# A hybrid decoder layer: block sums of right operands and the residual added by accumulating DMA on GpSimd's queue instead of VectorE

## The chip, the cores and the metric

The kernel runs on one core of one Trainium2 chip. The metric is the device time of one execution in microseconds (us). The engines are named as the profile names them: PE is TensorE (PEld its weight loads), DVE is VectorE, ACT is ScalarE, POOL is GpSimd, SP is SyncE, which here only issues DMAs. PSUM is the memory that TensorE writes, SBUF the working memory of 128 partitions. DMAs issued by SP are on the queue that the profile calls hardware_dynamic, those issued by POOL on the one called software_dynamic.

## The reference: what is computed

One layer of a decoder for one sequence of 1024 rows and a width of 2048, in float32, followed by a last RMSNorm. Cut to what matters here:

```python
h = rmsnorm(x, ln_g)                     # (1024, 2048)
proj = h @ w_in                          # one input projection, split into the groups' columns
out_a = gmlp_spatial_gating(g_u, g_v, ...) * silu(g_z)             # width 512
out_b = rmsnorm(gated_delta_rule(q, k, v, g, beta)) * silu(d_z)    # width 1024
out_c = cross_attention(c_q, mem) * silu(c_z)                      # width 512
mixed = concatenate([out_a, out_b, out_c])                         # (1024, 2048)
x = x + mixed @ w_out                    # the residual input is added here
return rmsnorm(x, final_g)
```

## The kernel before

**Precision and products.** Every large float32 product is made of three matmuls in the type float32r: each operand is split into a high part (a cast on ACT, `whi`, `zh` or `ahi`) and a low part (value minus high part, a subtraction on DVE, `wlo`, `zl` or `alo`), and `triple` adds high x high, high x low and low x high in PSUM.

**Order of the work.** Nothing is issued where it is written. Each call of an engine is recorded by `Plan.add` with what it depends on (reads and writes of tiles and DRAM tensors). `Plan.price` gives it a cost and, for DMAs, a size and a latency. `Plan.issue` then simulates the engines with these numbers and a rank (`with rank(...)`; smaller goes first) and emits the instructions in the order of the simulated start times. So all instructions carry the line of that emission, L274 in the profile, and each engine works through a fixed list in order. An instruction that waits holds up all that stand behind it on its engine; this goes for SP's and POOL's DMAs too.

**Stages.** The memory tokens' keys and values come first. Then come two passes (`half`) over the 512-row halves, which project q, k and v for the gated delta rule and run its chunked scan. Last come five products in block form, each made by `seven`: three input projections (`project_pair` 0, 1 and 2, for the gates, the queries and gMLP's u) and two output projections (`out_pair` 0 and 1, two 512-column blocks of `w_out` each).

**The block form.** The rows (two halves), the inner dimension (two halves of eight 128-blocks) and the columns (two 512-column blocks) give a 2 x 2 by 2 x 2 block product. `seven` computes it with seven block products instead of eight, from sums of blocks of the left operand (activations) and of the right one (weights). The products come in the order m = 1, 7, 6, 4, 5, 3, 2. Each runs over eight 128-blocks j in pairs, with four PSUM tiles t per block: 8 x 4 x 3 = 96 matmuls of 512 columns. After each product, `take1` to `take7` add what stands in PSUM to the results `y[half, column block]` on DVE. The left sums lie in DRAM (`s_d`); they were made in the background by `left_sums` and by `mix_done`, which adds on POOL.

**The right operand.** For `project_pair` 0 the sums of weight blocks are made ahead, in the background of the first `half`, by `right_sums` (L738). A job takes four 512-column blocks from `w_in` into four `zg` tiles (SP), makes four differences on DVE and stores them to `t_d` (SP). There are eight jobs, at rank 6, started at marks in the projections (`next_job`). For the other four block products `rights_made` (L1241) makes the sums as they are needed: it loads one weight block per j into one of two buffers `wraw2` (through `plain`). For m = 1, 2 and 3 that is the operand. For m = 7 it also loads block (1,1) into a kept tile and subtracts on DVE; for m = 6 it adds to the kept tile; for m = 4 and 5 it subtracts the kept tile from the loaded block, in the buffer. Then `split2` makes the high and low parts.

**Residual and norm.** In `out_pair`, `take6` and `take4` call `add_x` (L1470): a 512-column piece of x is loaded into one of six tiles (`xin`: the tiles `E` and `tn`) and added to `y` on DVE. `square` (ACT) sums the squares of a finished piece, `close` takes the root (a power on POOL), scales and stores the rows.

Of the kernel before, what the change touches and what calls it, by code (L numbers as in the profile page):

```python
# [17 lines left out]
P = 128  # L18
# [44 lines left out]
class Plan:  # L63
# [117 lines left out]
    def price(self, o, name, outs, ins):  # L181

        out = outs[0]
        n = math.prod(out.shape[1:])
        both = [*outs, *ins]
        psum = any(i.space == PSUM for i in both)
        pointer = any(i.shape[-1] == 1 and math.prod(i.shape[1:]) == 1 for i in ins[1:])
        o.nbytes = o.lock = 0
        o.lat = 0.0
        if name == "dma_start":  # L190
            o.cost = {"sp": 380.0, "act": 100.0, "pool": 800.0}[o.eng]
            rows = math.prod(out.shape[:-1])
            o.nbytes = max(4 * math.prod(out.shape), 512 * rows)
            src = ins[0]
            pieces = src.shape[-1] < 128 or out.shape[-1] < 128
            if out.space == DRAM:
                o.lat = 700.0 if pieces else 0.0
            elif pieces or list(src.ap)[0][0] == 0:
                o.lat = 2400.0
        elif o.eng == "pe":  # L200
            passes = 1 if ins[0].dtype == F32R else 2 if name == "transpose" else 4
            o.cost = max(13.3 + n / 2.4 * passes, 24.0 * out.shape[0] / 32 if out.shape[0] < P else 0.0)
            o.lat = 175.0
        elif o.eng == "act":
            o.cost = (165.0 if psum else 200.0) + 0.82 * n + (105.0 if pointer else 0.0)
            o.cost += 190.0 if "accum_out" in o.kw else 0.0
        elif o.eng == "dve":
            n = max([n] + [math.prod(i.shape[1:]) for i in ins])
            o.cost = (n + 151) / 0.96 + (60.0 if pointer and name == "scalar_tensor_tensor" else 0.0)
            o.lock = not psum and (name.startswith("tensor_") or name == "scalar_tensor_tensor")  # L210
            o.lock = o.lock and name != "tensor_reduce"
        else:
            o.lock = 1
            if name in ("memset", "affine_select"):
                o.cost = 100.0 + 0.83 * n * (1 if name == "memset" else 1.4)
            else:
                o.cost = 550.0 + 150.0 * (n - 1) if n < 8 else 200.0 + 2.1 * n
# [60 lines left out]
def kernel(  # L278
# [447 lines left out]
    def left_sums(src, dst):  # L726
        a, b, c, d = (ring["zg"]() for _ in range(4))
        with rank(6):
            for t, x_ in zip((a, b, c, d), src):
                Q.dma_start(t, x_)  # L730
            V.tensor_tensor(out=d, in0=c, in1=d, op=ALU.add)
            V.tensor_tensor(out=c, in0=a, in1=c, op=ALU.subtract)
            V.tensor_tensor(out=a, in0=d, in1=a, op=ALU.subtract)
            V.tensor_tensor(out=b, in0=b, in1=a, op=ALU.subtract)
            for t, x_ in zip((d, a, c, b), dst):
                Q.dma_start(x_, t)

    def right_sums(src, dst):  # L738
        a, b, c, d = (ring["zg"]() for _ in range(4))
        with rank(6):  # L740
            for t, x_ in zip((a, b, c, d), src):
                Q.dma_start(t, x_)
            V.tensor_tensor(out=a, in0=b, in1=a, op=ALU.subtract)
            V.tensor_tensor(out=b, in0=d, in1=b, op=ALU.subtract)
            V.tensor_tensor(out=d, in0=d, in1=a, op=ALU.subtract)
            V.tensor_tensor(out=c, in0=c, in1=d, op=ALU.subtract)
            for t, x_ in zip((a, d, b, c), dst):
                Q.dma_start(x_, t)

    def blk(w, k, c0):  # L750
        return w[k * P : (k + 1) * P, c0 : c0 + HT]
# [401 lines left out]
    ah4, al4 = (over([t.rearrange("p t k c -> p (t k c)")[:, i * 2 * HT : (i + 1) * 2 * HT] for t in ts for i in range(2)])  # L1153
                for ts in (ahq[0:2], alq[0:2]))
    wraw2 = over(kvraw[:2])
    more = [[ring["inv"]()]]
    whi3 = over([*kvhi, heir(zgb[0], "zh", "zg0", 2 * HT, F32R)])
    wlo3 = over([*kvlo, heir(zgb[1], "zl", "zg1", 2 * HT, F32R)])
    ywide = [heir(o, f"y{i}", tag)
# [20 lines left out]
                split_to(hi[:, i * n : (i + 1) * n], lo[:, i * n : (i + 1) * n], t, V)  # L1180
        return hi, lo

    def add(o, a, b):
        with rank(1):
            V.tensor_tensor(out=o, in0=a, in1=b, op=ALU.add)

    def seven(lefts, rights, banks, plan, order=range(NH), rows=False, last=False):

        for n, (m, take) in enumerate(plan):
# [22 lines left out]
                    product(t, *h)  # L1212
                take(t, bank[t])
            if n == 1:
                araw.bufs[1:] = more


    def lefts(blocks, s):
# [21 lines left out]

    def rights_made(blocks, kept):  # L1241


        def get(m, js):
            r = plain([blocks(*((0, 0), (1, 0), (1, 1), (1, 0), (1, 1), (0, 0), (0, 1))[m - 1], j) for j in js])
            if m < 4:
                return split2([r], whi3(), wlo3())
            ts = kept[js[0] // 2]
            if m == 7:
                with rank(4):  # L1250
                    for i, x_ in enumerate(js):
                        t = ts[i] if len(ts) == 2 else ts[0][:, i * HT : (i + 1) * HT]
                        Q.dma_start(t, blocks(1, 1, x_))
            with rank(2):
                for i, t in enumerate(ts):
                    n = t.shape[1]
                    x_ = r[:, i * n : (i + 1) * n]
                    if m in (4, 5):
                        V.tensor_tensor(out=x_, in0=x_, in1=t, op=ALU.subtract)
                    else:  # L1260
                        V.tensor_tensor(out=t, in0=t, in1=x_, op=ALU.subtract if m == 7 else ALU.add)
            return split2([r] if m in (4, 5) else ts, whi3(), wlo3())

        return get

# [8 lines left out]
    def project_pair(c, ys, done, kept=None, first=3):  # L1274

        y = {k: ys[4 * i : 4 * i + 4] for i, k in enumerate(KEYS)}

        def fin(key, t):
            with rank(first if key[0] == 1 else 3):
                done(*key, t, y[key][t])  # L1280

        def take1(t, a):
            with rank(1):
                S.copy(y[0, 0][t], a)

        def take7(t, a):
            add(y[1, 1][t], a, y[0, 0][t])

        def take6(t, a):
            add(y[1, 1][t], a, y[1, 1][t])  # L1290
            add(y[0, 1][t], a, y[0, 0][t])

        def take4(t, a):
            add(y[1, 0][t], a, y[1, 1][t])
            fin((1, 0), t)

        def take5(t, a):
            add(y[1, 1][t], a, y[1, 1][t])
            add(y[0, 1][t], a, y[0, 1][t])
            fin((1, 1), t)  # L1300

        def take3(t, a):
            add(y[0, 1][t], a, y[0, 1][t])
            fin((0, 1), t)

        def take2(t, a):
            add(y[0, 0][t], a, y[0, 0][t])
            fin((0, 0), t)

        def w_block(i, b, j):  # L1310
            return blk(w_in, NH * i + j, pairs[c][b])

        plan = ((1, take1), (7, take7), (6, take6), (4, take4), (5, take5), (3, take3), (2, take2))
        right = rights_made(w_block, kept) if kept else rights_kept(w_block, t_d)
        seven(lefts(h_block, s_d[0]), right, lambda n: wide, plan)


# [28 lines left out]
    def mix_done(hf, k, y):  # L1346
# [4 lines left out]
        with rank(6):  # L1351
            if hf == 0:
                Q.dma_start(a, s_d[1][j][1])
                G.tensor_tensor(out=a, in0=y, in1=a, op=ALU.subtract)
                Q.dma_start(s_d[1][j][3], a)
                return
            c, d = spare_t(), spare_t()
            Q.dma_start(a, mix_d[0][set1[j]])
            Q.dma_start(c, mix_d[1][set1[j]])
            G.tensor_tensor(out=d, in0=c, in1=y, op=ALU.add)  # L1360
            G.tensor_tensor(out=c, in0=a, in1=c, op=ALU.subtract)
            G.tensor_tensor(out=a, in0=d, in1=a, op=ALU.subtract)
            for i, t in enumerate((d, a, c)):
                Q.dma_start(s_d[1][j][i], t)

# [74 lines left out]
    fg = [t[:, i * HT : (i + 1) * HT] for t in fg for i in range(2)]  # L1440
    for c in range(4):
        Q.dma_start(fg[c], final_g[c * HT : (c + 1) * HT].partition_broadcast(P))
    xin = Ring("", 0, None)
    xin.bufs = ring["E"].bufs + ring["tn"].bufs
    ssy = [[small() for _ in range(NT)] for _ in range(2)]
    ys = [[[None] * 4 for _ in range(NT)] for _ in range(2)]

# [19 lines left out]
                    to = S  # L1467
            to.dma_start(out[r0 : r0 + P, c * HT : (c + 1) * HT], y)

    def add_x(half_, t, c, a=None):  # L1470
        y, r0 = ys[half_][t][c], half_ * HT + t * P
        xt = xin()
        Q.dma_start(xt, x[r0 : r0 + P, c * HT : (c + 1) * HT])
        add(y, y if a is None else a, xt)

    def square(half_, t, c):
        S.activation(jk, ys[half_][t][c], AF.Square, accum_out=ssy[half_][t][:, c : c + 1])
# [1 line left out]
    def out_pair(cp, slots, kept):  # L1479
# [11 lines left out]
            add(y[1, 1][t], a, y[0, 0][t])  # L1491

        def take6(t, a):
            add(y[1, 1][t], a, y[1, 1][t])
            add(y[0, 1][t], a, y[0, 0][t])
            add_x(0, t, c1)
            add_x(0, t, c2)

        def take4(t, a):
            add(y[1, 0][t], a, y[1, 1][t])  # L1500
            add_x(1, t, c2)
            add_x(1, t, c1)
            square(1, t, c1)

        def take5(t, a):
            add(y[1, 1][t], a, y[1, 1][t])
            add(y[0, 1][t], a, y[0, 1][t])
            square(1, t, c2)
            if cp == 1:
                close(1, t)  # L1510

        def take3(t, a):
            add(y[0, 1][t], a, y[0, 1][t])
            square(0, t, c2)
            G.tensor_tensor(out=y[0, 1][t], in0=y[0, 1][t], in1=fg[c2], op=ALU.mult)
            if cp == 1:
# [57 lines left out]
```

## Time and profile before

| what | value |
| --- | --- |
| median of 3 runs | 1705.58 us (1704.8 to 1708.16) |
| the profiled execution | 1705.49 us |
| its span, first to last instruction | 1703.8 us |
| mean granted TensorE clock | 0.995 |
| read from HBM, written | 310.59 MB, 87.06 MB |

The span is the time between the first and the last instruction of the profiled execution; that execution's own time lies 1.7 us above it. A busy time is the time in which an engine had an instruction under way. A matmul's end is modelled, and matmuls overlap, so TensorE's pace is better read from the number of matmuls in a stretch of time. The chain of waits follows the work that ended last backward, at each step to what released it. A window is a stretch of the span, in us from its start; the DMA share in it is the mean busy share of the core's 16 DMA engines.

### The profile page before, as it was taken

To read this page: it belongs to the slowest core of one execution; us is meant where nothing else is said; L and a number is where in the kernel's file an instruction comes from. 1 tells how busy PE (TensorE), PEld (TensorE's weight loads), DVE (VectorE), ACT (ScalarE), POOL (GpSimd) and SP (SyncE) were. 2 spreads that over 40 slices of the span, in tenths; PEclk is the share of its full clock that TensorE was granted. 3 is DMA by queue.
4 is the path that set the end of the run, shared out by engine and by line. 5 is a ranking of instruction groups with operands and counts; after the bars stand their busy time and mean duration, and the time that the engine had idled before them with its cause. 6 is when DMAs were issued, how large, how long until landed. Compare 5 with 4: busy or idle time off the path is not lost.

```text
span 1703.8 us, 26921 instructions
## 1 busy us (share of the span) xinstructions
PE 1674.5 (98%) x8861; PEld 1389.8 (82%) x8861; DVE 1323.5 (78%) x2478; ACT 910.7 (53%) x2010; POOL 179.0 (11%) x163
## 2 busy tenths in 40 slices
PE   8999999999999999999999999999999999899987
PEld 7888888888888888888888888888888888688876
DVE  5866897979875576858695687888987999767786
ACT  6763754657655655746563544345544443444344
POOL 0024100100001000000000000003100221011002
PEclk9999999999999999999999999999999999999999
DMA  7798888687665878768766697658858888766566
GB/s 256 219 305 283 244 285 235 191 243 224 191 175 175 247 212 244 225 162 280 214 192 202 226 327 263 197 186 262 289 181 279 278 298 279 250 205 225 186 195 249
DMA packets 332025, 399.49 MB, mean 234 GB/s; under 512 B 50862, under 2 KB 172391, under 8 KB 331884
## 3 DMA queue, kind: packets, MB, share of 16 engines
q1 hardware_dynamic: 330148, 394.60, 72.7%
q0 software_dynamic: 1120, 2.10, 0.5%
q8 instruction: 70, 1.15, 0.3%
q10 hardware_dynamic: 616, 1.07, 0.2%
q14 instruction: 71, 0.58, 0.1%
HBM read 310.59 MB, written 87.06 MB: 233 GB/s over the span
## 4 chain that ended last, share of the span: by engine, by line
PE 86%; DVE 6%; DMA 4%; ACT 1%; issue 1%; POOL 0%; SPq 0%; POOLq 0%; DVEq 0%; ACTq 0%
PE acc L274 69%; PE dn L274 17%; DVE y L274 1%; DMA wraw<-in_w_out_dram 1%; DMA wraw<-in_w_in_dram 1%; DVE wlo L274 1%; DVE alo L274 1%; DMA inv<-sd 1%; DVE wraw L274 1%; DMA E<-in_x_dram 0%; DVE tn L274 0%; DMA sd<-sp 0%; DMA sd<-y 0%; DVE vs L274 0%; DVE qT L274 0%
## 5 line engine op out<-in xcount | busy, mean ns | idle before, releaser
L274 PE MATMUL acc<-ahi,whi 128*128 128x512 f32 x1216 | 482.1, 397 | 0.3 <-ACT ahi L274 0.3
L274 PE MATMUL acc<-alo,whi 128*128 128x512 f32 x1216 | 481.9, 396 | 0.0
L274 PE MATMUL acc<-ahi,wlo 128*128 128x512 f32 x1216 | 481.6, 396 | 0.0
L274 ACT CAST whi<-wraw 128x512 fp32r<-128x512 f32 (+1 forms) x297 | 215.7, 727 | 251.6 <-PE acc L274 198.4
L274 PEld LDWEIGHTS acc<-ahi,wlo 128*128 128x128 f32 x1216 | 228.7, 188 | 44.3
L274 PEld LDWEIGHTS acc<-alo,whi 128*128 128x128 f32 x1216 | 228.7, 188 | 44.2 <-DVE alo L274 0.5
L274 PEld LDWEIGHTS acc<-ahi,whi 128*128 128x128 f32 x1216 | 228.6, 188 | 44.2 <-ACT ahi L274 0.5
L274 DVE TENSOR_TENSOR wlo<-wraw,whi 128x512 fp32r<-128x512 f32 (+1 forms) x201 | 180.5, 900 | 79.2 <-ACT whi L274 73.0
L274 PE MATMUL acc<-whi,ahi 128*128 128x512 f32 x280 | 110.7, 402 | 4.3 <-ACT whi L274 4.2
L274 PE MATMUL acc<-wlo,ahi 128*128 128x512 f32 x280 | 111.5, 398 | 0.7 <-DVE wlo L274 0.6
L274 PE MATMUL acc<-whi,alo 128*128 128x512 f32 x280 | 111.2, 398 | 0.0
L274 DVE TENSOR_TENSOR alo<-gt,ahi 128x1024 fp32r<-128x1024 f32 x70 | 87.7, 1253 | 20.9 <-ACT ahi L274 20.8
L274 ACT CAST ahi<-gt 128x1024 fp32r<-128x1024 f32 x70 | 73.4, 1048 | 49.8 <-PE acc L274 22.2
L274 DVE TENSOR_TENSOR alo<-inv,ahi 128x1024 fp32r<-128x1024 f32 x66 | 84.0, 1273 | 17.4 <-ACT ahi L274 17.3
L274 ACT CAST ahi<-inv 128x1024 fp32r<-128x1024 f32 x66 | 69.0, 1046 | 42.0 <-PE acc L274 20.4
L274 PE MATMUL acc<-ahi,zh 128*128 128x512 f32 x224 | 88.0, 393 | 0.0
L274 PE MATMUL acc<-ahi,zl 128*128 128x512 f32 x224 | 87.7, 391 | 0.0
L274 PE MATMUL acc<-alo,zh 128*128 128x512 f32 x224 | 87.6, 391 | 0.0
L274 POOL TENSOR_TENSOR hs<-hs,mhalf 128x4 f32<-128x4 f32 x32 | 37.4, 1169 | 449.3 <-DVE hs L274 449.3
L274 DVE TENSOR_TENSOR inv<-inv,y 32x31 f32<-32x31 f32 (+15 forms) x248 | 81.2, 327 | 3.6
L274 DVE TENSOR_TENSOR y<-inv,inv 32x31 f32<-32x31 f32 (+15 forms) x248 | 80.7, 325 | 3.4
L274 ACT CAST zh<-wraw 128x1024 fp32r<-128x1024 f32 x35 | 36.8, 1050 | 55.3 <-PE acc L274 28.3
(371 smaller groups left out, 3282.5 us busy)
## 6 DMA issues: line engine op xcount, KB each, us to landing
wraw<-in_w_in_dram SPq DMA_DIRECT2D x360, 256.0 KB
wraw<-in_w_out_dram SPq DMA_DIRECT2D x112, 256.0 KB
low<-wlo SPq DMA_DIRECT2D x96, 256.0 KB
wlo<-low SPq DMA_DIRECT2D x96, 256.0 KB
gt<-sd SPq DMA_DIRECT2D x80, 256.0 KB
inv<-sd SPq DMA_DIRECT2D x76, 256.0 KB
zg<-in_w_in_dram SPq DMA_DIRECT2D x32, 256.0 KB
td<-zg SPq DMA_DIRECT2D x32, 256.0 KB
```

The source lines that it names most:

```text
L274: o.fn(*o.args, **o.kw)
```

## The change

An accumulating DMA adds its source to what stands in its destination. It is issued on POOL's queue (`more`). It replaces DVE's additions in three places:

- `right_sums` works with two tiles instead of four. One gets b11, to which b12 is added. The other gets b22, to which b12, b11 and b21 are added one after the other, and the tile is stored after each step.
- `rights_made`: for m = 7, 6, 4 and 5 the operand is the kept tile itself. For m = 7 block (1,1) is loaded into it and (0,1) is added; for m = 6 (0,0) is added, for m = 4 (1,0). For m = 5 it is loaded anew with (0,0), and (0,1) is added. The buffer `wraw2` serves only m = 1, 2 and 3.
- `add_x`: x is added to `y` straight from DRAM; the tiles `xin` go.

Because this form of DMA only adds, the signs of the block form are turned: `left_sums`, `mix_done` and the `take` functions add where they subtracted or exchange their operands, with the same shapes. The planner gets a latency of 1500 ns more for an accumulating DMA, and its order changes everywhere with the new costs. The core of the diff:

```diff
@@ price
             o.nbytes = max(4 * math.prod(out.shape), 512 * rows)
+            o.lat = 1500.0 if "accum_op" in o.kw else 0.0
@@ left_sums (signs; mix_done on POOL in the same way)
-            V.tensor_tensor(out=d, in0=c, in1=d, op=ALU.add)
-            V.tensor_tensor(out=c, in0=a, in1=c, op=ALU.subtract)
-            V.tensor_tensor(out=a, in0=d, in1=a, op=ALU.subtract)
-            V.tensor_tensor(out=b, in0=b, in1=a, op=ALU.subtract)
+            V.tensor_tensor(out=d, in0=c, in1=d, op=ALU.subtract)
+            V.tensor_tensor(out=c, in0=a, in1=c, op=ALU.add)
+            V.tensor_tensor(out=a, in0=d, in1=a, op=ALU.add)
+            V.tensor_tensor(out=b, in0=a, in1=b, op=ALU.subtract)
...
+    def more(t, src):
+
+        G.dma_start(t, src, accum_op=ALU.add)
+
     def right_sums(src, dst):
-        a, b, c, d = (ring["zg"]() for _ in range(4))
+        b11, b12, b21, b22 = src
+        t, o = ring["zg"](), ring["zg"]()
         with rank(6):
-            for t, x_ in zip((a, b, c, d), src):
-                Q.dma_start(t, x_)
-            V.tensor_tensor(out=a, in0=b, in1=a, op=ALU.subtract)
-            V.tensor_tensor(out=b, in0=d, in1=b, op=ALU.subtract)
-            V.tensor_tensor(out=d, in0=d, in1=a, op=ALU.subtract)
-            V.tensor_tensor(out=c, in0=c, in1=d, op=ALU.subtract)
-            for t, x_ in zip((a, d, b, c), dst):
-                Q.dma_start(x_, t)
+            Q.dma_start(o, b11)
+            more(o, b12)
+            Q.dma_start(dst[0], o)
+            Q.dma_start(t, b22)
+            for x_, to in ((b12, dst[2]), (b11, dst[1]), (b21, dst[3])):
+                more(t, x_)
+                Q.dma_start(to, t)
@@ rights_made
+        PLAIN = {1: (0, 0), 2: (1, 0), 3: (1, 1)}
+        BASE = {7: (1, 1), 5: (0, 0)}
+        MORE = {7: (0, 1), 6: (0, 0), 4: (1, 0), 5: (0, 1)}
 
         def get(m, js):
-            r = plain([blocks(*((0, 0), (1, 0), (1, 1), (1, 0), (1, 1), (0, 0), (0, 1))[m - 1], j) for j in js])
-            if m < 4:
-                return split2([r], whi3(), wlo3())
+            if m in PLAIN:
+                return split2([plain([blocks(*PLAIN[m], j) for j in js])], whi3(), wlo3())
             ts = kept[js[0] // 2]
-            if m == 7:
-                with rank(4):
-                    for i, x_ in enumerate(js):
-                        t = ts[i] if len(ts) == 2 else ts[0][:, i * HT : (i + 1) * HT]
-                        Q.dma_start(t, blocks(1, 1, x_))
-            with rank(2):
-                for i, t in enumerate(ts):
-                    n = t.shape[1]
-                    x_ = r[:, i * n : (i + 1) * n]
-                    if m in (4, 5):
-                        V.tensor_tensor(out=x_, in0=x_, in1=t, op=ALU.subtract)
-                    else:
-                        V.tensor_tensor(out=t, in0=t, in1=x_, op=ALU.subtract if m == 7 else ALU.add)
-            return split2([r] if m in (4, 5) else ts, whi3(), wlo3())
+            with rank(4):
+                for i, j in enumerate(js):
+                    t = ts[i] if len(ts) == 2 else ts[0][:, i * HT : (i + 1) * HT]
+                    if m in BASE:
+                        Q.dma_start(t, blocks(*BASE[m], j))
+                    more(t, blocks(*MORE[m], j))
+            return split2(ts, whi3(), wlo3())
...
-    def add_x(half_, t, c, a=None):
-        y, r0 = ys[half_][t][c], half_ * HT + t * P
-        xt = xin()
-        Q.dma_start(xt, x[r0 : r0 + P, c * HT : (c + 1) * HT])
-        add(y, y if a is None else a, xt)
+    def add_x(half_, t, c):
+        r0 = half_ * HT + t * P
+        more(ys[half_][t][c], x[r0 : r0 + P, c * HT : (c + 1) * HT])
...
         def take6(t, a):
-            add(y[1, 1][t], a, y[1, 1][t])
-            add(y[0, 1][t], a, y[0, 0][t])
+            add(y[1, 1][t], y[1, 1][t], a, ALU.subtract)
+            add(y[0, 1][t], a, y[0, 0][t], ALU.subtract)
             add_x(0, t, c1)
             add_x(0, t, c2)
```

More of the change, by code (lines that the diff above doesn't have):

```diff
@@ L1155 @@
     wraw2 = over(kvraw[:2])
-    more = [[ring["inv"]()]]
+    spare_raw = [[ring["inv"]()]]
     whi3 = over([*kvhi, heir(zgb[0], "zh", "zg0", 2 * HT, F32R)])
@@ L1181, in split2, with add @@
         return hi, lo
-    def add(o, a, b):
+    def add(o, a, b, op=ALU.add):
         with rank(1):
-            V.tensor_tensor(out=o, in0=a, in1=b, op=ALU.add)
+            V.tensor_tensor(out=o, in0=a, in1=b, op=op)
     def seven(lefts, rights, banks, plan, order=range(NH), rows=False, last=False):
@@ L1214, in seven @@
             if n == 1:
-                araw.bufs[1:] = more
+                araw.bufs[1:] = spare_raw
     def lefts(blocks, s):
@@ L1289, in take6 @@
         def take6(t, a):
-            add(y[1, 1][t], a, y[1, 1][t])
-            add(y[0, 1][t], a, y[0, 0][t])
+            add(y[1, 1][t], y[1, 1][t], a, ALU.subtract)
+            add(y[0, 1][t], a, y[0, 0][t], ALU.subtract)
         def take4(t, a):
-            add(y[1, 0][t], a, y[1, 1][t])
+            add(y[1, 0][t], a, y[1, 1][t], ALU.subtract)
             fin((1, 0), t)
@@ L1298, in take5 @@
             add(y[1, 1][t], a, y[1, 1][t])
-            add(y[0, 1][t], a, y[0, 1][t])
+            add(y[0, 1][t], y[0, 1][t], a, ALU.subtract)
             fin((1, 1), t)
         def take3(t, a):
-            add(y[0, 1][t], a, y[0, 1][t])
+            add(y[0, 1][t], y[0, 1][t], a, ALU.subtract)
             fin((0, 1), t)
@@ L1353, in mix_done @@
                 Q.dma_start(a, s_d[1][j][1])
-                G.tensor_tensor(out=a, in0=y, in1=a, op=ALU.subtract)
+                G.tensor_tensor(out=a, in0=a, in1=y, op=ALU.subtract)
                 Q.dma_start(s_d[1][j][3], a)
@@ L1359, in mix_done @@
             Q.dma_start(c, mix_d[1][set1[j]])
-            G.tensor_tensor(out=d, in0=c, in1=y, op=ALU.add)
-            G.tensor_tensor(out=c, in0=a, in1=c, op=ALU.subtract)
-            G.tensor_tensor(out=a, in0=d, in1=a, op=ALU.subtract)
+            G.tensor_tensor(out=d, in0=c, in1=y, op=ALU.subtract)
+            G.tensor_tensor(out=c, in0=a, in1=c, op=ALU.add)
+            G.tensor_tensor(out=a, in0=d, in1=a, op=ALU.add)
             for i, t in enumerate((d, a, c)):
@@ L1442 @@
         Q.dma_start(fg[c], final_g[c * HT : (c + 1) * HT].partition_broadcast(P))
-    xin = Ring("", 0, None)
-    xin.bufs = ring["E"].bufs + ring["tn"].bufs
     ssy = [[small() for _ in range(NT)] for _ in range(2)]
@@ L1493, in take6 @@
         def take6(t, a):
-            add(y[1, 1][t], a, y[1, 1][t])
-            add(y[0, 1][t], a, y[0, 0][t])
+            add(y[1, 1][t], y[1, 1][t], a, ALU.subtract)
+            add(y[0, 1][t], a, y[0, 0][t], ALU.subtract)
             add_x(0, t, c1)
@@ L1499, in take4 @@
         def take4(t, a):
-            add(y[1, 0][t], a, y[1, 1][t])
+            add(y[1, 0][t], a, y[1, 1][t], ALU.subtract)
             add_x(1, t, c2)
@@ L1506, in take5 @@
             add(y[1, 1][t], a, y[1, 1][t])
-            add(y[0, 1][t], a, y[0, 1][t])
+            add(y[0, 1][t], y[0, 1][t], a, ALU.subtract)
             square(1, t, c2)
@@ L1512, in take3 @@
         def take3(t, a):
-            add(y[0, 1][t], a, y[0, 1][t])
+            add(y[0, 1][t], y[0, 1][t], a, ALU.subtract)
             square(0, t, c2)
```

## The prediction, made before the changed kernel ran

> **What bounds the kernel now.** I read the page first, then the windows table by stage, then the chain of waits where the table shows a loss. The first rows of the page, the queue rows under them, and a table of windows (us from the span's start; busy time of PE, PEld, DVE, ACT and POOL with instruction counts, then the granted clock, the DMA share and GB/s):
>
> ```profile
> span 1703.8 us, 26921 instructions
> PE 1674.5 (98%) x8861; PEld 1389.8 (82%) x8861; DVE 1323.5 (78%) x2478; ACT 910.7 (53%) x2010; POOL 179.0 (11%) x163
> q1 hardware_dynamic: 330148, 394.60, 72.7%
> q0 software_dynamic: 1120, 2.10, 0.5%
> ```
>
> ```profile
> 0.00:985.00 985.00, 976.71 (x5712) 814.53 (x5713) 732.70 (x1733) 577.62 (x1522) 100.15 (x111) 1.00 0.74 228
> 985.00:1437.80 452.80, 451.94 (x2094) 375.41 (x2093) 392.26 (x492) 218.77 (x326) 54.87 (x32) 1.00 0.77 257
> 1437.80:1490.60 52.80, 46.74 (x195) 36.96 (x194) 44.26 (x52) 21.05 (x29) 0.00 (x0) 0.97 0.77 250
> 1490.60:1599.40 108.80, 108.80 (x481) 90.12 (x481) 72.42 (x82) 49.63 (x69) 12.02 (x8) 1.00 0.60 198
> 1599.40:1650.60 51.20, 46.78 (x193) 37.14 (x193) 42.64 (x53) 19.88 (x27) 0.00 (x0) 0.93 0.68 216
> 1650.60:1703.80 53.20, 43.47 (x192) 35.67 (x190) 39.27 (x71) 23.75 (x41) 12.00 (x12) 0.94 0.68 238
> ```
>
> TensorE is busy for 98% of the span, so taking work off VectorE pays only where TensorE waits. The fourth window is TensorE undisturbed: 108.8 us / 481 = 0.2262 us for each 512-column matmul. A stage of `seven` is 8 blocks x 4 tiles x 3 matmuls = 96, or 21.7 us. At that pace the 195 matmuls of the third window need 44.1 us and take 52.8: 8.7 us lost. The 193 of the fifth need 43.7 and take 51.2: 7.5 us lost. Part of each loss is idle time, part a lower granted clock (0.97 and 0.93) just after it. Elsewhere there is little: 8.3 us idle in the first 985 us, 0.9 in the next 453. In the last window 9.8 us are mostly the tail after the last matmul, which this change leaves alone.
>
> The two lossy windows are products m=4 and m=5 of the two output pairs. The chain of waits through them, in order of time (start, length, what):
>
> ```profile
> 1445.16 5.41 DMA wraw<-in_w_out_dram
> ...
> 1450.69 1.24 DVE wraw L274
> ...
> 1454.78 5.51 DMA wraw<-in_w_out_dram
> ...
> 1460.41 1.23 DVE wraw L274
> 1461.64 0.60 DVE kd L274
> ```
>
> ```profile
> 1606.79 1.14 DVE wraw L274
> ...
> 1620.94 1.21 DVE y L274 x2
> ...
> 1622.34 6.50 DMA E<-in_x_dram
> ...
> 1629.48 1.82 DVE wraw L274 x2
> ```
>
> In the first, the two `wraw` buffers go round: load (5.4 to 5.5 us), VectorE subtract, cast and split, and only then the next load. VectorE also takes the additions of `take4` and `add_x` (kd, vs) in between. In the second, VectorE's queue stands behind an addition of the residual whose input takes 6.50 us to land; the subtraction for m=5 (wraw) is queued behind it. All of these instructions are in the edit.
>
> **The change part by part.** *VectorE.* The groups that go, with mean ns (the `zg` groups hold the left sums too, so half of them stays):
>
> ```profile
> L274 DVE TENSOR_TENSOR y<-y,wraw 128x1024 f32<-128x1024 f32 x16 | 20.5, 1286 | 0.5 <-DMA wraw<-in_w_in_dram 0.5
> L274 DVE TENSOR_TENSOR wraw<-wraw,y 128x1024 f32<-128x1024 f32 x16 | 19.4, 1220 | 8.4 <-DMA wraw<-in_w_out_dram 5.4 <-DMA wraw<-in_w_in_dram 3.0
> L274 DVE TENSOR_TENSOR y<-y,tn 128x512 f32<-128x512 f32 x18 | 11.8, 682 | 0.1
> L274 DVE TENSOR_TENSOR zg<-zg 128x512 f32<-128x512 f32 x32 | 21.8, 682 | 2.3 <-DMA zg<-hTd 1.6 <-DMA zg<-in_w_in_dram 0.5
> ```
>
> Pair 1 and output pair 0 lose the 32 wide additions of the first two rows (39.9 us). Pair 2 and output pair 1 lose 8 more wide ones (at 1.22 us, 9.8) and 48 of 512 columns (at 0.68, 33). The residual loses 32 at 0.682 (22 us), `right_sums` 32 at 0.682 (22 us). That is some 127 us of VectorE's 1323.5. Where TensorE is full this is worth nothing. In the third window it takes away 8 subtractions at 1.22 and 16 residual additions at 0.68, 20.7 of 44.26 busy us.
>
> *The stall.* In m=4 to 7 the right operand no longer passes through `wraw`. It grows in the kept tile, and its addition may be issued as soon as the previous product's split has read that tile: about one stage, 21.7 us, ahead. Product 5 needs a base load and then an addition. With 5.5 us (the longer `wraw` load above) for the one and 6.5 for the other, 12.0 us, it still fits. So I take both losses as gone: -16.2 us. Next late would be the left operands, 8 loads a stage, which keep their two buffers.
>
> *The new DMAs.* By the code there are 32 (`right_sums`) + 4 x 4 x 8 = 128 (`rights_made`) + 32 (`add_x`) = 192 accumulating DMAs of 256 KB, all on POOL's queue. On SP's queue there are 32 more base loads for m=5 and 192 fewer loads of addends. In `right_sums` b12 and b11 are now read twice (16 loads more in all). No accumulating DMA is in this trace; the nearest rows are the plain loads that POOL issues, grouped, and their landing:
>
> ```profile
> L274 POOL DMA_DIRECT2D ai<-kvd x4 | 2.4, 601 | 53.6 <-PE dn L274 53.5
> DMA to landing us min/median/max: 2.9/3.1/4.0
> ```
>
> Issuing costs POOL 0.60 us: 192 x 0.6 = 115 us, beside its 179 busy us in 1704. Landing, from issue: at least 2.9 us; 6.5 us (the residual load above) at the busy end; I take 3.1, as the same queue shows it, with one more pass of 256 KB at about 400 GB/s (0.65 us). For the DMA engines I count an accumulating DMA as k plain ones: k=1 if the second read is hidden, k=3 if reading, adding and writing back are three passes. I take 2.
>
> The bound on the sum of passes, from the best tenths of one window in GB/s, and the stretches where the additions fall:
>
> ```profile
> GB/s 407 412 381 407 401 408 384 378 374 280 340 404 400 404 410 386 388 300 10 46 309 225 186 341 295 229 403 396 411 399 377 381 374 194 0 37 311 276 101 303
> 130.00:500.00 370.00, 368.43 (x2126) 308.38 (x2125) 312.57 (x782) 211.60 (x617) 47.13 (x38) 1.00 0.75 230
> 1282.00:1434.00 152.00, 151.60 (x703) 125.38 (x702) 137.28 (x154) 70.78 (x93) 30.54 (x18) 1.00 0.85 289
> 1434.00:1686.00 252.00, 241.52 (x1040) 196.68 (x1039) 194.11 (x238) 108.04 (x149) 21.82 (x16) 0.98 0.66 216
> ```
>
> At 400 GB/s, 1282 to 1434 carries 60.8 MB. It moves 289 x 152 = 43.9 now and gets 2.1 of base loads and, by the new order on POOL, some 56 accumulating DMAs: at k=2 another 14.7, together 60.7. That is full to the brim but not over. 1434 to 1686, shortened by 16, carries 94.4 MB and needs 54.4 + 4.2 + 96 x 0.262 = 83.8. So at k=2 nothing is added, though latencies rise.
>
> The Trainium skill, "Collectives: The Full Stack", section "The bandwidth ceiling: the fold count and why AG ≠ RS ≠ AR", says that a reduction in the DMA path is slower not through the add itself but because it needs two source reads. By that rule k is 2 and the sum stays as it is; no run here shows it yet.
>
> *right_sums.* Before, one job is four loads, four additions, four stores. Now it is a chain on two tiles: each addition waits for the store of what stands in the tile, each store (SP) for the addition. SP and POOL work in order; queued behind are the `wraw` loads on SP and the `hs` powers on POOL. The jobs lie at 130 to 500, where TensorE idles 1.57 us (370 less 368.43). The cover is four `wraw` pieces of 12 matmuls, 4 x 12 x 0.2262 = 10.9 us. From below it is 0 (a gain is excluded, TensorE being full), from above the rival below; I take a doubling of that idle time, +1.6 us.
>
> *The switch from one pair to the next.* There POOL's sums, SP's stores behind them and the next pair's loads follow each other without slack:
>
> ```profile
> 1190.55 2.17 POOL y L274
> 1192.74 5.34 DMA sd<-y
> ...
> 1209.16 5.75 DMA sd<-sp
> 1215.85 5.34 DMA inv<-sd
> ```
>
> In the new order on POOL the first additions of pair 2 (kd, vs) stand between these sums, and each waits for its base load. POOL is held, then SP's store, then the loads behind that. At least 0; at most one landing of 6.5 us at each of two switches, 13; I take one landing of the queue's own, +3.1.
>
> *The signs* (operand order, add for subtract, also POOL's sums) keep every instruction's size: nothing. The planner's new `lat` changes the order alone.
>
> *Sum.* The profiled execution took 1705.49 us, 1703.8 of it span, and stands at the median of the runs (1705.58). 1705.5 - 16.2 + 1.6 + 3.1 = **1694.0 us**.
>
> **The rivals.**
> 1. *The DMA engines become the bound* (slower). For it: 1282 to 1434 is already at a share of 0.85, and POOL's plain packets cost more of the engines' time than SP's: 0.5% of the span for 1120 packets against 72.7% for 330148, twice as much a packet, at larger packets. Against it: the later stages are at 0.60 to 0.68. It decides from k above 2 in pair 2 and 2.4 in the output pairs. At k=2.5, pair 2 needs 68 MB (170 us, +18) and the output pairs 96.4 (241 us, +5): 1717 us. At k=3 it is 75.4 MB (188 us, +36) and 109 (272 us, +36): 1766.
> 2. *SP is held by the chain of right_sums* (slower). 32 stores wait for additions. If those land more than the cover of 10.9 us later than their place in the order allows, each delay goes through to TensorE: a quarter of 32 landings of 3.1 us is 25 us, 1719. Against it: the loads quoted here land in 3 to 6.5 us.
> 3. *ScalarE takes VectorE's place* (no change). `square` in `take4` now waits for an accumulating DMA, in order ahead of the casts. 8 additions are issued together (8 x 0.6 us) and land in 6.5 or later, 11 us after the last addition in PSUM. If ScalarE stands for 6 us in each output pair, 12 of the 16.2 come back: 1706.
> 4. *The additions aren't on the queue in time* and m=5 stays exposed as before: the same 1702 to 1709.
>
> **How the numbers follow.** Forecast (1687 to 1702): 0.60. Rivals 3 and 4 together: 0.12. Rival 1: 0.18. Rival 2: 0.10. The forecast's own low end is 1705.5 - 16.2 less the idle time that may go with it (0.9 and 1.6): 1687; its high end the costs at 13 instead of 3.1, near 1702. The range reaches to k=2.5 and most of rival 2: **1687 to 1718**, which leaves out the dearer half of the rivals. A measurement of this kernel can tell about 0.2%, 3.4 us, from no change: faster 0.60, same 0.12, slower 0.28.
>
> **What will show it.** Right: the two windows of m=4 and 5 take about 44 us for their matmuls at clock 1.00, VectorE's busy time falls to near 1200 us, and no `wraw` load stands in the chain there except in m=1 to 3. The step on the queue is right if accumulating DMAs land in under 6.5 us; the step on passes if pair 2's DMA share stays under 1. Wrong: TensorE's idle time grows at 130 to 500 with SP waiting for DMA zg (rival 2); the DMA share sits at 0.95 or more in pair 2 with ScalarE waiting for loads (rival 1); ScalarE's `jk` waits for DMA y (rival 3).

## The result and the profile after

The changed kernel takes **1733.99 us** (median of 4 runs, 1731.11 to 1738.76) against 1706.87 for the kernel before in the same comparison. The ratio is 1.0162, 95% interval 1.0132 to 1.0192: slower by 1.6%, where 1694.0 was forecast and 1718 was the upper end of the range. The profiled execution took 1731.70 us at a mean granted clock of 0.993. The same rows of its page as were shown of before:

```profile
span 1730.0 us, 26907 instructions
PE 1680.9 (97%) x8861; PEld 1391.4 (80%) x8861; DVE 1217.3 (70%) x2338; ACT 912.0 (53%) x2022; POOL 347.7 (20%) x355
...
q1 hardware_dynamic: 309412, 356.84, 64.6%
q0 software_dynamic: 28768, 52.44, 17.4%
```

VectorE lost 106 us of work, as was wanted, and the span grew by 26.2 us. The new entry is the last row: POOL's queue moves 52.44 MB and takes 17.4% of the DMA engines' time, 301 us of 1730. SP's queue moves 356.84 MB in 64.6%. Per megabyte POOL's packets cost 1.83 times as much (5.74 us against 3.13).

To place the loss I lined up the traces by the k-th of the 6400 large matmuls (those with a high or a low part among their operands). The table gives how many us later it starts than in before, at the time that it had before; e1 and e9 are experiments told below. They have the order of after, so after can be set against them directly; against before, some matmuls have changed places.

| at, in before | after | e1 | e9 | what ends there |
| --- | --- | --- | --- | --- |
| 500 us | 7.7 | 1.3 | 3.7 | the stretch with right_sums |
| 1182 us | 10.7 | 1.4 | 4.9 | pair 1 |
| 1382 us | 17.7 | 0.3 | 3.5 | pair 2 |
| 1438 us | 27.1 | 4.3 | 7.7 | m=1, 7 and 6 of output pair 0 |
| 1494 us | 26.7 | -4.7 | -1.3 | m=4 and 5 of output pair 0 |
| 1600 us | 26.7 | -4.7 | -1.4 | the undisturbed stretch |
| 1637 us | 19.0 | -12.4 | -9.0 | m=5 of output pair 1 |
| the last | 24.3 | -12.4 | -9.0 | the end |

(The opening 43 us give 1.7 in after and 2.0 in e9, before any accumulating DMA, so that is scatter of the start.) After loses some 6 us where `right_sums` runs, 3 up to the end of pair 1, 7 in pair 2 and 9 in the first three products of output pair 0. In m=4 and 5 of output pair 0 it neither loses nor gains (52.2 us against 52.5 in before and 43.5 in e1): the forecast gain isn't there. It gains 7.7 in output pair 1, of which 5 are lost again behind it. The first large matmul of output pair 0 starts at 1371.8 us in before, so the stretch from 1282 to 1434 that the prediction calls pair 2 belongs to output pair 0 from there on. The windows of after around these places, with the columns of the prediction's table (the last three are clock, DMA share and GB/s):

```profile
1200.00:1300.00 100.00, 95.24 (x455) 79.09 (x454) 72.27 (x118) 51.51 (x108) 41.20 (x40) 0.97 1.04 286
1427.20:1470.50 43.30, 35.99 (x152) 27.76 (x152) 27.83 (x27) 15.40 (x16) 21.55 (x22) 1.00 0.97 257
1470.50:1513.80 43.30, 37.69 (x155) 30.30 (x154) 16.47 (x16) 13.94 (x18) 13.20 (x15) 0.92 1.08 255
1455.00:1710.00 255.00, 244.40 (x1060) 199.94 (x1059) 150.32 (x173) 109.64 (x155) 77.83 (x80) 0.99 0.85 222
```

In the first three, where TensorE stands idle, the DMA share is at about 1 (above 1 I read it as "full"), and the rate is 255 to 286 GB/s, not the 400 of the prediction. The last row, in which most of the output pairs' work lies, averages 0.85: the mean doesn't show it. VectorE is busy for only 28 and 16 of 43 us there. The chain of waits of after through output pair 0 says what TensorE waits for:

```profile
1418.52 6.42 DMA sd<-sp
1424.94 0.02 issue
1424.96 10.62 DMA inv<-sd
...
1455.37 5.78 DMA y<-in_w_out_dram
...
1462.33 19.00 DMA y<-in_w_out_dram x2
1481.33 0.02 issue
1481.35 12.98 DMA inv<-sd
...
1494.43 1.05 ACT ahi L275
```

Two loads of a left operand (`inv<-sd`) take 10.62 and 12.98 us; the prediction's chain showed one of 5.34 in before. Two DMAs on the weights, one after the other, take 19.00: an addition that POOL issues at 1462.33 and a base load that SP issues at 1470.63, as the addition lands. By the chain SP issues the second `inv<-sd` only when that base load is in. So the loss comes to TensorE by SP's queue, which stands behind slow landings, and by the slow landing of the left operand itself. The `wraw` loads that stood in the chain of m=4 and 5 in before are gone. ScalarE's casts of the left operands show the same thing summed over the whole kernel (busy, mean ns | idle time before them, what ended it); first before, then after:

```profile
L274 ACT CAST ahi<-gt 128x1024 fp32r<-128x1024 f32 x70 | 73.4, 1048 | 49.8 <-PE acc L274 22.2 <-PE dn L274 17.8 <-DMA gt<-h0d 5.8
L274 ACT CAST ahi<-inv 128x1024 fp32r<-128x1024 f32 x66 | 69.0, 1046 | 42.0 <-PE acc L274 20.4 <-DMA inv<-mixd 10.6 <-PE dn L274 7.2
```

```profile
L275 ACT CAST ahi<-gt 128x1024 fp32r<-128x1024 f32 x70 | 73.4, 1048 | 67.6 <-DMA gt<-sd 31.0 <-PE acc L275 11.0 <-PE dn L275 10.3
L275 ACT CAST ahi<-inv 128x1024 fp32r<-128x1024 f32 x66 | 69.1, 1046 | 61.2 <-DMA inv<-sd 26.0 <-DMA inv<-mixd 14.7 <-PE dn L275 8.3
```

In before the casts waited mostly for TensorE, which is what a kernel bound by TensorE looks like; in after they wait for loads from `s_d`, 31.0 and 26.0 us.

### The profile page after: what moved, and what is told of

Read it like the earlier page. It is cut to its first block, busy times and chain, and to the rows that moved or that the text cites. A ratio compares the mean times of both kernels' runs of the same rounds, so it can differ in the third digit from the quotient of the medians.

```text
span 1730.0 us, 26907 instructions
## 1 busy us (share of the span) xinstructions
PE 1680.9 (97%) x8861; PEld 1391.4 (80%) x8861; DVE 1217.3 (70%) x2338; ACT 912.0 (53%) x2022; POOL 347.7 (20%) x355
## 3 DMA queue, kind: packets, MB, share of 16 engines
q1 hardware_dynamic: 309412, 356.84, 64.6%
q0 software_dynamic: 28768, 52.44, 17.4%
q10 hardware_dynamic: 616, 1.07, 0.2%
## 5 line engine op out<-in xcount | busy, mean ns | idle before, releaser
L275 ACT CAST whi<-wraw 128x512 fp32r<-128x512 f32 (+1 forms) x276 | 193.8, 703 | 199.3 <-PE acc L275 160.2
L275 DVE TENSOR_TENSOR wlo<-wraw,whi 128x512 fp32r<-128x512 f32 (+1 forms) x180 | 155.0, 862 | 85.8 <-ACT whi L275 79.8
L275 POOL DMA_DIRECT2D zg<-in_w_in_dram x32 | 29.2, 935 | 184.6 <-DMA td<-zg 118.5
```

The source lines that it names most:

```text
L275: o.fn(*o.args, **o.kw)
```

## The experiments

**Theory A**: an accumulating DMA takes about two plain passes of the DMA engines' time. Where many come together, the engines are full, and SP's loads of the left operands land late. **Rival B**: not the engines' time but the queues in order. POOL and SP stand while additions wait for base loads and stores for additions, and issuing is dear. **Rival C**: the planner's new order (the new costs and 1500 ns) is bad in itself, whatever the DMAs cost.

### e1: the same order, plain copies

The 192 additions become plain copies from the same place to the same tile; the planner is given the same costs, so the order and every wait remain.

```diff
-            o.lat = 1500.0 if "accum_op" in o.kw else 0.0
+            o.lat = 1500.0 if o.eng == "pool" and ins[0].tensor.name.startswith("in_") else 0.0
...
-        G.dma_start(t, src, accum_op=ALU.add)
+        G.dma_start(t, src)
```

> The changed kernel with its 192 additions issued as plain copies of the same 256 KB from the same queue (the sums are left out: what lands overwrites the tile). Order, waits and tiles are those of the changed kernel; only what the DMA engines do for each DMA differs. Theory A (the DMA engines' time: a packet of an accumulating DMA takes them about twice as long as a plain one, and where many are queued the other loads land late): most of the loss goes, 1695 to 1705 us, plain packets on POOL's queue near 100 ns instead of 176, and loads of sd no longer take 10 us. Theory B (the chains on two in-order queues: base load, POOL's wait, addition, SP's store behind it): the chains are unchanged, so 1722 us or more. Theory C (the planner's new order by itself): also unchanged, 1722 or more.

Measured: 1698.0 us (8 runs), ratio 0.9954 (0.9942 to 0.9967), span 1693.1. The same order is 36 us faster once nothing is added. Its queue row and two windows:

```profile
q0 software_dynamic: 16480, 52.44, 9.9%
```

```profile
1200.00:1300.00 100.00, 100.00 (x494) 83.81 (x493) 74.51 (x118) 51.57 (x106) 29.41 (x41) 1.00 0.91 311
1434.00:1530.00 96.00, 96.00 (x425) 79.54 (x424) 59.20 (x64) 45.76 (x64) 20.91 (x30) 1.00 0.74 242
```

With the same 52.44 MB POOL's queue takes 168 us of the engines (9.9% of 1693) instead of 301. Without the 8.5 us of its other loads (0.5% of the span in before) that is 292 against 159: **k = 1.84**. The time is as theory A expected, its packets are not: a plain one takes 163 ns on average, not 100, against 167 in after, since the same bytes go in 16480 packets instead of 28768. TensorE is full in both windows. The casts in e1:

```profile
L275 ACT CAST ahi<-gt 128x1024 fp32r<-128x1024 f32 x70 | 73.4, 1048 | 63.3 <-PE dn L275 24.2 <-PE acc L275 22.6 <-DMA gt<-sd 8.6
L275 ACT CAST ahi<-inv 128x1024 fp32r<-128x1024 f32 x66 | 69.1, 1047 | 44.9 <-DMA inv<-sd 12.4 <-PE dn L275 12.1 <-DMA inv<-mixd 11.7
```

The wait for left operands falls from 57 us (31.0 and 26.0) to 21 (8.6 and 12.4). Rival C is out as the main cause: every engine works through the same instructions in the same order as in after. A small part may be the order's: e1 and e9 both lose some 4 us between 1382 and 1438. Rival B is weakened but not out, since plain copies are also issued and land sooner.

### e2, e3, e4: one part alone

Each puts two of the three parts back on VectorE with the turned signs; the changed lines are those of the diff above, reversed with the signs (m=5 subtracts the block from the kept tile).

> Only the residual is added by accumulating DMA (32 of the 192); block sums on VectorE as before, with turned signs. Theory A: 32 accumulating DMAs are a small load, in four bursts of 8; the wait for the residual's load on VectorE goes, but each burst delays other loads: 1698 to 1708 us. Theory B: no base loads and no stores hang on these additions, so nothing new is waited for: 1695 to 1700. Theory C: anything.

> Only the right operands' sums in rights_made by accumulating DMA (128 of the 192); residual and right_sums on VectorE. Theory A: the switch to pair 2 still loses some 8 us and output pair 0 loses less than in the changed kernel, since the residual's bursts are gone: 1710 to 1722 us. Theory B: the base load, addition and mixing chains are all still there: 1722 to 1730.

> Only right_sums by accumulating DMA (32 of the 192, with its chain of stores). The changed kernel is 5.3 us later than before at 500 us, so both theories say 1709 to 1714 us; by theory B SP stands waiting for zg additions (some 38 us in the changed kernel), by theory A the DMA share in 170 to 300 us rises from 0.84 to 0.97. A time near 1706 would say that the 5 us belong to something else.

Measured, against 1705.64 for before: the residual alone 1709.42 (ratio 1.0023, 1.0008 to 1.0039), `rights_made` alone 1722.72 (1.0102, 1.0084 to 1.0119), `right_sums` alone 1709.25 (1.0022, 1.0009 to 1.0034). The parts cost 3.8, 17.1 and 3.6 us, 24.5 together of the whole's 27. So most of the loss hangs on `rights_made`, the part with 128 of the 192 DMAs and the one that was to bring the gain. These three times don't decide between the theories. e2 is slower than both said (by 1.4 us for A, by 9 for B), e3 lies 0.7 above A's range and inside B's, and e4 is where both put it, with the signs of both: SP waits 38.5 us for `zg` additions, and the share in 170 to 300 us is 0.95 (0.83 in before). In e3 the two stretches look as in after:

```profile
1200.00:1300.00 100.00, 91.96 (x439) 75.64 (x438) 70.21 (x114) 46.04 (x100) 38.23 (x38) 0.97 1.04 286
1434.00:1530.00 96.00, 84.76 (x349) 68.15 (x350) 67.97 (x74) 39.95 (x50) 16.24 (x17) 0.93 0.84 241
```

### e9: the same kind, the same waits, half the bytes

The recorded call issues only the first 256 of the 512 columns of source and tile; what the planner sees, and so the order, stays.

```diff
-        G.dma_start(t, src, accum_op=ALU.add)
+        issue, h = nc.gpsimd.dma_start, HT // 2
+        G.dma_start(t, src, accum_op=ALU.add).fn = lambda a, b, **k: issue(a[:, 0:h], b[:, 0:h], **k)
```

> The changed kernel in the same order, but each accumulating DMA adds only the first 256 of its 512 columns (the other half of each sum is left out). The additions keep their kind, their place, their waits and what hangs on them; their bytes and so about half of the DMA engines' time for them go. Theory A (engine time): near the plain copies of e1, 1696 to 1708 us. Rival (what costs is the accumulating DMA as such: its issue and its latency beside a plain one): little changes, 1722 us or more.

Measured: 1694.32 us (4 runs), ratio 0.9938 (0.9921 to 0.9954), span 1694.6.

```profile
PE 1672.1 (99%) x8861; PEld 1389.8 (82%) x8861; DVE 1214.2 (72%) x2338; ACT 912.0 (54%) x2022; POOL 343.6 (20%) x355
...
q0 software_dynamic: 28768, 27.28, 10.8%
```

```profile
1200.00:1300.00 100.00, 100.00 (x494) 83.96 (x493) 75.86 (x120) 52.91 (x108) 42.05 (x43) 1.00 0.98 270
1434.00:1530.00 96.00, 96.00 (x425) 79.51 (x424) 57.86 (x62) 45.66 (x61) 27.16 (x28) 1.00 0.78 213
```

These are real accumulating DMAs, as many packets (28768), in the same order with every wait, and POOL is as busy as in after (343.6 against 347.7 us). Only the bytes, and with them the engines' time (10.8%, 183 us), are fewer. The time is 1.7 us under theory A's range: the loss is gone and nearly the whole forecast gain is there. That speaks against rival B as a cause of its own: neither the issue on POOL nor the same waits cost the 40 us once there are fewer bytes. What it can't separate is the DMA engines' time from what each addition's own landing gains by being smaller (for tile `y` the median falls from 7.3 to 5.9 us). Note also that 0.98 for 100 us is still borne here; it is at 1.04 that after lost.

### e5: no addition, but the second pass

Plain copies as in e1, and behind each one a second plain copy of the same 256 KB to DRAM tiles that nobody reads.

```diff
-        G.dma_start(t, src, accum_op=ALU.add)
+        to, issue = aside.pop(), nc.gpsimd.dma_start
+        G.dma_start(t, src).fn = lambda *a: (issue(*a), issue(to, a[1]))
```

> The order of the changed kernel, its additions as plain copies (as in e1, so the sums are left out), and behind each copy POOL issues a second plain copy of the same 256 KB into a DRAM tile that nobody reads and nobody waits for. Theory A (engine time: what costs is the second pass, whoever makes it): the 1698 us of e1 go back to between 1720 and 1745. Rival (it is the addition's own latency, issue to landing, that the chains wait for, not the engines' time): the extra copy is waited for by nobody, so 1698 to 1706.

Measured: 1758.23 us (4 runs), ratio 1.0302 (1.0285 to 1.032).

```profile
q0 software_dynamic: 31840, 102.79, 17.6%
```

17.6% of 1758 is 309 us, nearly after's 301, with no accumulation at all, and the kernel loses 60 us against e1, 13 more than theory A's range allowed. The copies that are waited for, plain as in e1, land later too (median for tile `y` 6.2 us against 5.0). So the engines' time suffices for a loss. It is not a measure of its size: after loses 36 against e1 at the same engine time. A write to DRAM is not the write back into the tile, and POOL issues twice.

### e10: the signs alone

All additions on VectorE and SP's queue as before, only the signs turned.

> All additions back on VectorE and the residual's tiles back, only the signs of the block form turned: the order of the instructions is that of the kernel before. Both theories: 1704 to 1708 us, no difference.

Measured: 1705.37 us (10 runs), ratio 1.0002 (0.9991 to 1.0013). The signs cost nothing that can be measured.

### e7: the planner told of the second pass

```diff
+            o.nbytes *= 2 if "accum_op" in o.kw else 1
```

> The changed kernel, but the planner counts two passes for an accumulating DMA (524 KB instead of 262). Same instructions, other order. Theory A says that the engines' work stays and only its spacing can change: 1720 to 1738 us. If the order was the fault (the planner put left loads behind bursts that it took for short), most of it returns: below 1712.

Measured: 1775.66 us (4 runs), ratio 1.0412 (1.0391 to 1.0432). Neither range holds: an order planned with two passes is 42 us worse than after's. Why was not settled; the order changes in too many places. So order does matter by this much, but e1 and e9 show that the order of after isn't what lost the most.

### e6 and e8: what is left of the idea

e6 keeps `right_sums` and `rights_made` on VectorE and gives only the residual to POOL, as an addition of two tiles; no DMA accumulates.

```diff
-        add(y, y, xt)
+        G.tensor_tensor(out=y, in0=y, in1=xt, op=ALU.add)
```

> No accumulating DMA at all: block sums on VectorE, the residual loaded by SP as before and added by POOL (32 tensor_tensor of 1.3 to 2 us) instead of VectorE. If VectorE's queue behind the residual's load is what costs in the output pairs, the 7.5 us of the second one go and part of the 8.7 of the first: 1694 to 1700 us. If it was the round of the wraw buffers that bound, 1702 to 1707.

Measured: 1697.75 us (4 runs), ratio **0.9955** (0.994 to 0.997). It beats both kernels. Lined up by the same matmuls it gains 4.5 us up to the undisturbed stretch and 7.2 more in output pair 1 (1.3 of them are lost again at its end), the places where the prediction saw the residual's additions in VectorE's queue.

e8 adds to e6 accumulating DMAs only for m=4 and 5 of the output pairs, the place with the two losses (2 pairs x 2 products x 8 blocks = 32 DMAs).

> Accumulating DMA only for m=4 and 5 of the two output pairs (32 of 192), where the chain of before stands; the residual is added by POOL; all other sums on VectorE. Theory A: a small load in a stretch whose DMA share is 0.60 to 0.77, so it should do no harm, and both stalls of before go: 1690 to 1697 us. If even these few additions hold up the left loads: 1700 or more.

Measured: 1711.04 us (5 runs), ratio 1.0037 (1.0023 to 1.0051): 13 us worse than e6, and against what theory A expected. Its chain through output pair 0:

```profile
1433.31 8.95 DMA inv<-mixd
...
1443.42 4.86 DVE alo L275
...
1448.67 10.64 DMA inv<-mixd
...
1468.96 9.14 DVE alo L275
```

Two loads of left operands are late again: the DMA share from 1430 to 1460 us is 1.09, though the expectation went by means of 0.60 to 0.77. And two subtractions on VectorE are under way for 4.86 and 9.14 us while POOL adds the residual (below). So e8 doesn't measure the DMAs alone, but it gives no ground for keeping them even there.

## Why the prediction was wrong, step by step

**The failed step: "So at k=2 nothing is added."** The second passes do add: after is 36 us slower than e1, which has the same order without them. The factor itself was well chosen. Over the whole kernel k is 1.84 by after and e1. In one bad stretch, 1400 to 1520, it can be read from one view, the queues of a window (packets, MB, share of the 16 engines); first after, then e1:

```profile
q0 software_dynamic: 6192, 11.27, 53.0%
q1 hardware_dynamic: 10346, 18.84, 45.1%
```

```profile
q1 hardware_dynamic: 11936, 21.74, 52.8%
q0 software_dynamic: 3078, 10.07, 26.6%
```

In after POOL's 11.27 MB take more of the engines than SP's 18.84: 53.0% of 120 us is 5.64 us a megabyte against 2.87, a factor of 1.96. The packets of the two queues have the same mean size there (1.82 KB), so small packets don't explain it. In e1 the two queues are nearly alike, 3.17 and 2.91. The Trainium skill's rule from "Collectives: The Full Stack", section "The bandwidth ceiling: the fold count and why AG ≠ RS ≠ AR", that a reduction needs a second read, agrees with these numbers; the profile shows the time, not the read. It was the use made of k that failed, in three ways:

- *The capacity.* 400 GB/s was read from the best tenths. The quoted rows gave a lower one: 289 GB/s at a share of 0.85 is 340 at full share, 216 at 0.66 is 327. With these, pair 2's 60.7 MB take 178.5 us instead of 152, and the output pairs' 83.8 MB 256 instead of 236: +46 us, 1740. At k = 1.84 the second passes are 16% less, 58.3 and 79.8 MB, and the same sum gives +20 and +8, 1722. The measured 1734 lies between, but that is partly luck, since the places don't fit: in the sum all but 4.7 us of the loss lies in these two stretches, while against e1 after loses 17 us ahead of 1282 (some 3 of them scatter of the start), 5 in the first stretch and 14 in the second. Rival 1 was the right mechanism with its threshold put too high, "k above 2".
- *The place.* The sum put some 56 additions into the first stretch and 96 into the second. In the like stretches of after (1300 to 1455 and 1455 to 1710) POOL issues 30 and 64. Another 32 lie from 1192 to 1300, which the sum left out, and the share there is 1.04.
- *The average.* The sum was over 152 and 252 us. The additions come in bursts (11.27 MB at 0.262 each are 43 of the 192 in these 120 us), and the left operands have only their two buffers of slack. Over 1455 to 1710 the share is only 0.85, yet there are 43-us stretches at 0.97 and 1.08 in it or just ahead of it. There the loads named as "next late" were late.

**The gain, 16.2 us: the mechanism and the size were right, but after has only part of it.** With less for the engines to do (e1 and e9) TensorE gets 9.0 us in m=4 and 5 of output pair 0 (8.7 forecast; the two take 43.5 us in e1) and 7.7 in output pair 1 (7.5 forecast). But both lose some 4 us just ahead of the first, in m=7 and 6, which the prediction didn't have, so that 12.7 are left in e1. After has the 7.7 too, but not the 9.0.

**VectorE** fell by 106 us, not 127 (1323.5 to 1217.3). The instructions that went held 127 us one by one, as forecast; but 14 us of that were overlap with neighbours, which busy time counts once, and the rest took some 6 us longer. It decided nothing.

**The landing was taken too short**: 3.75 us (3.1 and 0.65), with 6.5 as upper bound. The landing times of the accumulating DMAs into tile y and tile zg in after, and of e1's plain copies into y:

```profile
DMA to landing us min/median/max: 4.0/7.3/15.1
DMA to landing us min/median/max: 4.0/6.3/8.0
```

```profile
DMA to landing us min/median/max: 2.9/5.0/8.4
```

The least is 4.0, near the 3.75; the medians lie about the bound. That broke the sum of 12.0 us for a base load and an addition ("it still fits"): the chain showed 19.00 for two such DMAs.

**The issue on POOL** was taken at 0.60 us; 192 x 0.6 = 115. The groups of after and e1 for the residual and one for the weights:

```profile
L275 POOL DMA_DIRECT2D y<-in_w_out_dram x32 | 28.8, 1070 | 58.9 <-DMA y<-in_w_out_dram 26.0 <-DVE wlo L275 13.5 <-DVE alo L275 13.2
...
L275 POOL DMA_DIRECT2D y<-in_x_dram x16 | 15.9, 2107 | 0.0
```

```profile
L275 POOL DMA_DIRECT2D y<-in_w_out_dram x32 | 17.3, 542 | 66.7 <-DMA y<-in_w_out_dram 32.6 <-DVE wlo L275 12.6 <-ACT ahi L275 9.3
...
L275 POOL DMA_DIRECT2D y<-in_x_dram x16 | 8.5, 537 | 2.6 <-DVE y L275 1.8 <-DMA y<-in_x_dram 0.4 <-DMA gt<-in_w_out_dram 0.2
```

By the means a plain one takes 0.54, an accumulating one 1.07, and 2.1 for the residual's. But accumulating ones overlap in a burst, where most start 0.54 us apart; by busy time they take 0.90 (28.8 / 32) and 0.99 (15.9 / 16). POOL's busy time grew by 169 us in all. e9, with POOL as busy, shows that this isn't what cost the time.

**right_sums**: 1.6 us forecast, 6 measured in after by the matmuls' table (3.6 as the time of e4). Rival 2's sign is there, but small:

```profile
SPq L275 <- DMA zg<-in_w_in_dram: 38.3, 17, 6.9
```

SP waits 38.3 us in 17 waits, most of it covered. **The switch** to pair 2: 3.1 forecast, about 7 measured, and in e1 and e9 nothing is left of it. So the order alone doesn't cost it; it comes with the share of 1.04.

**Rival 3** was seen too, behind the loss in output pair 1: the chain of after has ScalarE's `jk` waiting for the residual.

```profile
1628.23 7.10 DMA ai<-in_w_out_dram
1635.39 15.94 DMA gt<-in_w_out_dram
...
1655.09 13.59 DMA y<-in_x_dram
1668.76 0.07 ACT jk L275
```

It was priced at 6 us a pair, and it is the likely place of the 5 us that after loses there; e1 and e9, with the same waits, don't lose them. So it looks like a consequence of A and not a cause of its own.

**Still open**: whether the full resource is the DMA engines' own time or something that lengthens their packets (the profile gives packets' times, not their reason); how much of the loss is the late landing of the additions themselves, with SP's queue behind them, and how much that of the other loads; why e1 and e9 lose 4 us ahead of m=4; why e7's order is so much worse; and how much of e8's loss is the collision on VectorE.

## What to carry to other kernels

Price an accumulating DMA at two plain passes of the DMA engines (1.84 to 1.96 here), and lay that against the capacity that the stage's own row shows (GB/s divided by its share), in the busiest 40 to 100 us and not in the stage's mean. Then ask which small, punctual loads share the engines there, and what stands behind the additions in the queues: in this kernel it was the loads of the left operands that came late. When TensorE is at 98%, taking 106 us from VectorE is worth only what stands in the chain of waits; moving the residual's additions to a nearly idle engine (e6) brought 7.6 us, about half of the forecast gain, without a byte more.

## What the runs showed of the hardware that was not expected

- With the same bytes plain copies from POOL went in 16480 packets and accumulating DMAs in 28768; the granularity differs beside the second pass. Plain copies on SP's queue have the smaller packets too and cost half as much a megabyte (above).
- An addition of two tiles on POOL slows VectorE's while both run. The timeline of e6 (start, length, engine, operation):

```profile
1471.22 2.28 POOL L275 TENSOR_TENSOR kd<-kd,E 128x512 f32<-128x512 f32 x1
1472.26 2.31 DVE L275 TENSOR_TENSOR alo<-inv,ahi 128x1024 fp32r<-128x1024 f32 x1
...
1482.63 1.22 DVE L275 TENSOR_TENSOR alo<-inv,ahi 128x1024 fp32r<-128x1024 f32 x1
```

The same subtraction takes 2.31 us beside POOL and 1.22 alone; in e8 one was under way for 9.14 us. The Trainium skill, "SBUF — State Buffer", section "Who interferes with whom", says that a VectorE instruction with two SBUF inputs contends with GpSimd's reads; the trace agrees. e6 wins in spite of it.
